# Both parts of the mixing stage's weight tiles made by transfers instead of ACT and DVE

## The chip, the cores and the metric

The kernel runs on one core of one Trainium2 chip. The metric is the time of one execution on the device in microseconds (us). A core has TensorE (PE, its weight loads shown as PEld), VectorE (DVE), ScalarE (ACT), GpSimd (POOL) and SyncE (SP). Each runs its own instructions in the order in which they stand, and waits on semaphores for the others. SP, ACT and POOL can issue transfers (DMAs); these run on 16 shared transfer engines.

## The reference

One decoder layer on 512 tokens of width 1024. Two token mixers run in parallel on the normalised input `h`: a sparse attention A, whose keys are the best 128 per query by an indexer's score, and a stick-breaking attention B. Both are gated, merged and projected, and a squared-ReLU MLP follows.

```python
h = rmsnorm(x, g_pre_mix[l]) * (1.0 + sc1) + sh1
proj = h @ w_in[l]
qa, ka, va, qb, kb, vb, qi, ki, wi, gate_a, gate_b = jnp.split(proj, split_at, axis=-1)
...
oa, ob = token_mixers(qa, ka, va, qb, kb, vb, qi, ki, wi)
merged = sigmoid(gate_a) * (oa @ w_up_a[l]) + sigmoid(gate_b) * (ob @ w_up_b[l])
x = x + ga1 * rmsnorm(merged @ w_out[l], g_post_mix[l])
...
u = relu(h @ w_ff1[l])
x = x + ga2 * rmsnorm((u * u) @ w_ff2[l], g_post_ffn[l])
```

## The kernel before

**Three products for one.** Matrices are multiplied in TensorE's `fp32r` format, which keeps fewer bits than fp32. To keep precision, each operand is split into a high part (the value rounded to fp32r) and a low part (what the rounding left), and `mm3` adds three products: high by high, high by low, low by high. `split` makes the parts: ACT copies the fp32 source into the high tile (a line of its own, L109), and DVE subtracts the high tile from the source into the low tile (L110).

**Weight tiles.** A weight tile is 128 partitions by up to 1024 columns, 512 KB. `wload` issues its load on SP's queue into a staging buffer `st` (three buffers) and splits it into `whi` and `wlo`, for each of which there are four buffers (`WBUF = 4`). A buffer is free when TensorE has done its last matmul with the tile four places earlier.

**The stages.** From 0 to 58 us the first stage multiplies `h` with `w_first` (indexer queries and keys and a part of V). Then comes the mixing stage, with 30 weight tiles in the order of the list `srcs`: six tiles of V weights (`w_v`) in two groups of three (V1 to V3 and V4 to V6: 876, 876 and 584 columns), and then, in the order of the string `ORDER`, two tiles (one of queries, one of keys) for each `b`, one for each `g` (gates), and four for each `a`. A group of V weights is used whole for each of four token blocks in turn, so its three buffers come free only in the last block. `wnext` hands out the next tile and calls `wload` for one tile ahead (`AHEAD = 1`). After the mixing stage, `srcs` goes on with the other gate tiles, `w_up` and `w_out`, and the MLP follows.

**What runs beside.** Into this stream of projections the generator tasks weave the indexer (scores, then 16 rounds of MAX and MATCH_REPLACE on DVE for the top-k), attention B (scores on TensorE; two sigmoids `a` and `be` on ACT; on DVE a scan of `a` and the product into `be`; transposes back on TensorE; `pT` evacuated by ACT) and later attention A. POOL makes masks and the three `affine_select`s on the indexer's scores `isc`, nothing else.

**Order.** The first stage's order is written by hand. In the mixing stage the order on each engine comes from a scheduler that works with its own estimates of durations; an engine then keeps to that order, whatever really comes late.

Of the kernel before, what the change touches and what calls it, by code (L numbers as in the profile page):

```python
# [7 lines left out]
F32 = mybir.dt.float32  # L8
F32R = mybir.dt.float32r
BF16 = mybir.dt.bfloat16  # L10
AF = mybir.ActivationFunctionType
ALU = mybir.AluOpType
# [3 lines left out]
D = 1024  # L16
# [45 lines left out]
def layer_kernel(tc, x, ada, vecs, c_row, rope, w_first, w_v, w_b, w_a, w_gate, w_up, w_out, w_ff1, w_ff2, out):  # L62
    nc = tc.nc
    es = ExitStack()
    with es:
# [5 lines left out]
        def uid(name):  # L71
            cnt[0] += 1
            return f"{name}_{cnt[0]}"
# [29 lines left out]
        def stage(src, w=D):  # L103
            st = per.tile([P, D], F32, name=uid("st"), tag="st", bufs=3)
            nc.sync.dma_start(st[:, :w], src)
            return st

        def split(dst_hi, dst_lo, src):
            nc.scalar.activation(dst_hi, src, AF.Copy)  # L109
            nc.vector.tensor_tensor(dst_lo, src, dst_hi.bitcast(F32), op=ALU.subtract)  # L110
# [1 line left out]
        wmore = []  # L112
        turn, wturn = [0], [0]

        def wload(src, w=D):
            st = stage(src, w)
            pool, tag, nb = per, "", WBUF
            if wmore:
                wturn[0] = (wturn[0] + 1) % (WBUF + 1)
                if wturn[0] == 0:  # L120
                    pool, tag, nb = wmore[0], "x", 1
            hi = pool.tile([P, D], F32R, name=uid("whi"), tag="whi" + tag, bufs=nb)
            lo = pool.tile([P, D], F32R, name=uid("wlo"), tag="wlo" + tag, bufs=nb)
            split(hi[:, :w], lo[:, :w], st[:, :w])
            return hi, lo

        def scaled_gain(dst, j, g0):
# [134 lines left out]
        for k in range(KT):  # L262
            if k + 1 < KT:
                prepare(k + 1)
            hi, lo = wfirst[k]
# [223 lines left out]
        srcs = [(w_v[g, i, :, :(k1 - k0) * VREST], (k1 - k0) * VREST) for g in range(2) for i, (k0, k1) in enumerate(V_CUTS)]  # L489
        feeds = {"b": iter(w_b[i] for i in range(8)), "g": iter(w_gate[i] for i in range(8)), "a": iter(w_a[i] for i in range(8))}  # L490
        for kind in ORDER:
            srcs += [(next(feeds[kind]), D) for _ in range({"b": 2, "g": 1, "a": 4}[kind])]
        for m in range(KT):
            srcs += [(w_gate[KT + m], D), (w_up[m], D)]
        srcs += [(w_out[k], D) for k in range(WOB)]
        ready = []

        def wnext(i=[0]):
            while len(ready) < min(len(srcs), i[0] + 1 + AHEAD):
                ready.append(wload(*srcs[len(ready)]))  # L500
            i[0] += 1
            return ready[i[0] - 1]

# [10 lines left out]
        def pair_b(hp):  # L514
            qq = q_pair()
            kk = k_pair()
            ps = yield from cols_T(wnext())
            for e in range(2):
                r, o = slice(e * HD, (e + 1) * HD), slice((1 - e) * HD, (2 - e) * HD)
                nc.scalar.activation(qq[r, e], ps[r], AF.Copy, scale=QK_SCALE)  # L520
                nc.vector.scalar_tensor_tensor(qq[o, e], ps[r], QK_SCALE, qq[r, e].bitcast(F32), op0=ALU.mult, op1=ALU.subtract)  # L521
            yield
            ps = yield from cols_T(wnext())
            for e in range(2):
                r, o = slice(e * HD, (e + 1) * HD), slice((1 - e) * HD, (2 - e) * HD)
                nc.scalar.activation(kk[r, 2 * e], ps[r], AF.Copy)
                nc.scalar.activation(kk[o, 2 * e + 1], ps[r], AF.Copy)
                nc.vector.tensor_tensor(kk[r, 2 * e + 1], ps[r], kk[r, 2 * e].bitcast(F32), op=ALU.subtract)
                evac(kk[o, 2 * e], kk[r, 2 * e + 1].bitcast(F32))
            yield  # L530
            tens[f"b{hp}"] = [(qq[:, e], kk[:, 2 * e:2 * e + 2]) for e in range(2)]

        def project(dst, scale):
            ws = [wnext(), wnext()]
            for t in range(NT):
                ts = slice(t * P, (t + 1) * P)
                ps = bank("mm")
                for k in range(KT):
                    hi, lo = ws[k // 4]
                    cs = slice((k % 4) * 256, (k % 4 + 1) * 256)  # L540
                    mm3(ps[:, :256], hTh[k][:, ts], hTl[k][:, ts], hi[:, cs], lo[:, cs], k == 0, k == KT - 1)
                    if k == 3:
                        yield
                nc.scalar.activation(dst[:, t], ps[:, :256], AF.Copy, scale=scale)  # L544
                if t == NT - 1:
                    do_rope(dst.rearrange("p t (h d) -> p t h d", h=4), 4)
                yield
# [104 lines left out]
        for m in range(KT):  # L652
# [3 lines left out]
            hi, lo = wnext()  # L656
# [50 lines left out]
        for k in range(KT):  # L707
            if k < WOB:
                wo.append(wnext())
            else:  # L710
                st = stage(w_out[k])
                hi = wp.tile([P, D], F32R, name=f"woh{k}")
                lo = wp.tile([P, D], F32R, name=f"wol{k}")
# [78 lines left out]
        def ff1(m, w, t0, t1):  # L792
# [8 lines left out]
            nc.vector.tensor_tensor(u2[m][:, cs], u2[m][:, cs], u2[m][:, cs], op=ALU.mult)  # L801

        ws = [wload(w_ff1[m]) for m in range(EARLY)]
        for h in range(2):
            for m in range(EARLY):
                ff1(m, ws[m], 2 * h, 2 * h + 2)
        for m in range(EARLY, MF):
            ff1(m, wload(w_ff1[m]), 0, NT)
            if m % 2 and m >= MF - 2 * KT:
                i = (m - MF + 2 * KT) // 2  # L810
                ada_cols(40 + i)
                gated_gain(KT + i, 40 + i, 72 + i)
# [106 lines left out]
```

## Time and profile before

| | |
|---|---|
| median of 3 runs | 812.72 us (812.08 to 813.03) |
| profiled execution | 811.92 us, its span 810.1 us |
| PE busy | 786.3 us, 97% of the span |
| DVE busy | 511.0 us, 63% |
| ACT busy | 363.0 us, 45% |
| POOL busy | 2.8 us |

The span runs from the first to the last instruction of the profiled execution; times in rows count from its start. An engine that is busy 97% on average can still stand in one stage, so the windows of a stage say more than the average. In a row `out<-in` names the written and the read tiles, and the bracket at its end gives the idle time before it and what ended it. A matmul's row shows a longer time than its distance to the next, since matmuls overlap.

### The profile page before, as it was taken

Reading aid. Unit: us, or ns where it says so; the run is one execution under the profiler, and the core shown is the slowest. Engines: PE = TensorE matmul, PEld = TensorE weight load, DVE = VectorE, ACT = ScalarE, POOL = GpSimd, SP = SyncE. Lnnn points to the kernel's source line nnn. Section 1 sums busy time; section 2 is a strip of 40 time slices with the busy share of each in tenths; the row PEclk is TensorE's granted clock in tenths of the full one; section 3 lists DMA queues with packets and bytes.
Section 4 is the critical chain, followed back from the end, with each engine's and each line's share of the span. In section 5 each row is a group of like instructions: output and inputs, shape, how many; then the busy total and the mean of one; then the engine's idle time right before and its main releaser. Section 6 shows DMA issues by size and latency. Waiting matters only on the chain.

```text
span 810.1 us, 10809 instructions
## 1 busy us (share of the span) xinstructions
PE 786.3 (97%) x4110; PEld 656.4 (81%) x4110; DVE 511.0 (63%) x973; ACT 363.0 (45%) x684; POOL 2.8 (0%) x15
## 2 busy tenths in 40 slices
PE   6999999989999999999999999999999999999996
PEld 5889977658889887887688998888888888888885
DVE  6876799999956776788767863344433433333325
ACT  6555657464546677631347753223322322332322
POOL 0000000000000000000000000000000000000000
PEclk9999999999999999999999999999999999999999
DMA  9933201122121210578780332344442232233202
GB/s 356 377 117 104 78 27 53 56 75 79 60 98 53 79 53 27 163 264 256 248 315 28 123 127 89 131 138 137 141 156 99 83 105 89 93 104 104 79 1 104
DMA packets 27987, 98.58 MB, mean 122 GB/s; under 512 B 3360, under 2 KB 3360, under 8 KB 27936
## 3 DMA queue, kind: packets, MB, share of 16 engines
q1 hardware_dynamic: 27216, 96.82, 35.2%
q10 hardware_dynamic: 720, 1.08, 0.4%
q8 instruction: 32, 0.52, 0.3%
q14 instruction: 19, 0.16, 0.1%
HBM read 95.79 MB, written 2.10 MB: 121 GB/s over the span
## 4 chain that ended last, share of the span: by engine, by line
PE 76%; DVE 15%; DMA 6%; issue 2%; ACT 2%; DVEq 0%; SPq 0%; ACTq 0%
PE mm L137 30%; PE s L137 27%; PE o L137 9%; PE tr L137 7%; DMA st<-in_ada_dram 3%; DVE a L483 3%; DVE isc L409 2%; DVE sm L408 2%; DVE wlo L110 2%; DMA st<-in_w_up_dram 2%; PE tr L427 1%; DVE be L485 1%; DVE st L210 1%; PE tr L333 1%; DVE qT L521 1%
## 5 line engine op out<-in xcount | busy, mean ns | idle before, releaser
L109 ACT ACTIVATE whi<-st 128x1024 fp32r<-128x1024 f32 (+2 forms) x122 | 127.5, 1047 | 180.8 <-PE mm L137 45.3
L110 DVE TENSOR_TENSOR wlo<-st,whi 128x1024 fp32r<-128x1024 f32 (+2 forms) x122 | 147.1, 1209 | 92.2 <-ACT whi L109 91.9
L137 PE MATMUL mm<-hTh,whi 128*128 128x512 f32 x192 | 78.7, 410 | 0.1
L110 DVE TENSOR_TENSOR ul<-u,uh 128x512 fp32r<-128x512 f32 x32 | 22.2, 692 | 89.7 <-ACT uh L109 89.6
L137 PE MATMUL mm<-hTh,wlo 128*128 128x512 f32 x192 | 75.6, 394 | 0.0
L137 PE MATMUL mm<-hTl,whi 128*128 128x512 f32 x192 | 75.4, 393 | 0.0
L109 ACT ACTIVATE uh<-u 128x512 fp32r<-128x512 f32 x32 | 20.2, 631 | 108.7 <-PE o L137 105.1
L137 PE MATMUL mm<-whi,hTh 128*128 128x256 f32 (+2 forms) x208 | 62.3, 306 | 0.1
L137 PE MATMUL mm<-whi,hTl 128*128 128x256 f32 (+2 forms) x208 | 60.2, 296 | 0.0
L137 PE MATMUL mm<-wlo,hTh 128*128 128x256 f32 (+2 forms) x208 | 60.1, 295 | 0.0
L210 DVE CUSTOM_DVE_ANT_0 st<-st,cb,vec 128x1024 f32<-128x1024 f32 x32 | 40.9, 1282 | 29.1 <-DMA st<-in_ada_dram 29.0
L137 PE MATMUL s<-h2h,whi 128*128 128x512 f32 (+1 forms) x144 | 52.7, 366 | 0.0
L137 PE MATMUL s<-h2l,whi 128*128 128x512 f32 (+1 forms) x144 | 52.6, 366 | 0.0
L137 PE MATMUL s<-h2h,wlo 128*128 128x512 f32 (+1 forms) x144 | 52.6, 366 | 0.0
L137 PEld LDWEIGHTS mm<-hTh,wlo 128*128 128x128 f32 x192 | 36.3, 189 | 7.8
L137 PEld LDWEIGHTS mm<-hTh,whi 128*128 128x128 f32 x192 | 36.5, 190 | 6.6 <-DVE qT L521 0.3
L137 PEld LDWEIGHTS mm<-hTl,whi 128*128 128x128 f32 x192 | 36.5, 190 | 6.2
L137 PEld LDWEIGHTS mm<-wlo,hTh 128*128 128x128 f32 x208 | 39.5, 190 | 1.0
L137 PEld LDWEIGHTS mm<-whi,hTl 128*128 128x128 f32 x208 | 39.5, 190 | 0.6
L137 PEld LDWEIGHTS mm<-whi,hTh 128*128 128x128 f32 x208 | 39.0, 190 | 0.7 <-ACT ka L544 0.3
L137 PE MATMUL mm<-h2h,wlo 128*128 128x512 f32 (+1 forms) x96 | 35.7, 372 | 0.0
L137 PE MATMUL mm<-h2h,whi 128*128 128x512 f32 (+1 forms) x96 | 35.7, 371 | 0.0
(296 smaller groups left out, 1755.1 us busy)
## 6 DMA issues: line engine op xcount, KB each, us to landing
st<-in_w_ff_dram SPq DMA_DIRECT2D x64, 512.0 KB, 3.3
st<-in_ada_dram SPq DMA_DIRECT2D x32, 512.0 KB, 4.2
sa<-in_ada_dram SPq DMA_DIRECT2D x16, 512.0 KB, 8.1
st<-in_w_gate_dram SPq DMA_DIRECT2D x16, 512.0 KB, 3.3
st<-in_w_first_dram SPq DMA_DIRECT2D x8, 512.0 KB, 8.5
st<-in_w_b_dram SPq DMA_DIRECT2D x8, 512.0 KB, 3.3
st<-in_w_a_dram SPq DMA_DIRECT2D x8, 512.0 KB, 3.2
st<-in_w_up_dram SPq DMA_DIRECT2D x8, 512.0 KB, 4.3
```

The source lines that it names most:

```text
L109: nc.scalar.activation(dst_hi, src, AF.Copy)
L110: nc.vector.tensor_tensor(dst_lo, src, dst_hi.bitcast(F32), op=ALU.subtract)
L137: nc.tensor.matmul(o, lhsT, rhs, start=start, stop=stop)
L210: nc.vector.tensor_tensor_reduce(out=st, in0=st, in1=cb[0], scale=1.0, scalar=vec[:, j:j + 1], op0=ALU.mult, op1=ALU.add, accum_out=mod[:, ...
L333: nc.tensor.transpose(ps[:, t * P:(t + 1) * P], s[:, t, i:i + 2].rearrange("p a d -> p (a d)"), identr)
L408: nc.vector.max(out=m8, in_=cur)
L409: nc.vector.match_replace(out=cur, in_to_replace=m8, in_values=cur, imm_value=SENT)
L427: nc.tensor.transpose(tr[:, j * P:(j + 1) * P], ps[e][:, j * P:(j + 1) * P], ident)
L483: nc.vector.tensor_tensor_scan(a[:, n - 1::-1], a[:, n - 1::-1], zero.to_broadcast([P, n]), 1.0, op0=ALU.mult, op1=ALU.add)
L485: nc.vector.tensor_tensor(be[:, :n - 1], be[:, :n - 1], a[:, 1:n], op=ALU.mult)
L521: nc.vector.scalar_tensor_tensor(qq[o, e], ps[r], QK_SCALE, qq[r, e].bitcast(F32), op0=ALU.mult, op1=ALU.subtract)
```

## The change

For the 30 tiles of the mixing stage `wload` takes another way. POOL issues a transfer from DRAM straight into the high tile, which casts fp32 to fp32r. ACT writes the negated high tile into the low tile. POOL issues a second transfer of the same source into the low tile that adds, so that source minus high stands there. No staging buffer, no load on SP and no subtraction on DVE belong to these tiles any more. All other tiles stay as they were. In `wnext` the tile's place in the list (`n_mixing` is 30) chooses the way.

```diff
-        def wload(src, w=D):
-            st = stage(src, w)
+        def wload(src, w=D, by_dma=False):
             pool, tag, nb = per, "", WBUF
...
             hi = pool.tile([P, D], F32R, name=uid("whi"), tag="whi" + tag, bufs=nb)
             lo = pool.tile([P, D], F32R, name=uid("wlo"), tag="wlo" + tag, bufs=nb)
-            split(hi[:, :w], lo[:, :w], st[:, :w])
+            if by_dma:
+                nc.gpsimd.dma_start(hi[:, :w], src)
+                nc.scalar.activation(lo[:, :w], hi[:, :w].bitcast(F32), AF.Copy, scale=-1.0)
+                nc.gpsimd.dma_start(lo[:, :w], src, accum_op=ALU.add)
+            else:
+                st = stage(src, w)
+                split(hi[:, :w], lo[:, :w], st[:, :w])
             return hi, lo
...
+        n_mixing = len(srcs)
...
-                ready.append(wload(*srcs[len(ready)]))
+                ready.append(wload(*srcs[len(ready)], len(ready) < n_mixing))
```

The order of instructions moves at two places that matter here. The first is POOL's queue around the V weights. Before, POOL had these rows from the start masks on:

```order
L94 MEMSET zero 128x1
L96 MEMSET eps 128x1
L344 MEMSET mask 128x128
L345 AFFINE_SELECT mask<-mask 128x128
L402 AFFINE_SELECT isc_585<-isc_585 128x128 x3
L915 UNCONDITIONAL_BRANCH
```

Now (`whi_614`, `whi_619`, `whi_624` are V1 to V3, and the `wlo` numbers one higher are their low parts; `629` and `823` are V4 and V5):

```order
L96 MEMSET eps 128x1
L124 DMA whi_614<-in_w_v_dram 128x876
L124 DMA whi_619<-in_w_v_dram 128x876
L126 DMA wlo_615<-in_w_v_dram 128x876
L349 MEMSET mask 128x128
L350 AFFINE_SELECT mask<-mask 128x128
L126 DMA wlo_620<-in_w_v_dram 128x876
L124 DMA whi_624<-in_w_v_dram 128x584
L126 DMA wlo_625<-in_w_v_dram 128x584
L124 DMA whi_629<-in_w_v_dram 128x876
L126 DMA wlo_630<-in_w_v_dram 128x876
L124 DMA whi_823<-in_w_v_dram 128x876
```

The high part of V3 stands behind the low part of V2, which in turn waits for ACT's negation. At the same place on ACT, at the end of the first stage, these rows stood before (`whi_622` is V2, `whi_628` is V3; `qi` evacuates the first stage's sums):

```order
L109 ACTIVATE whi_616<-st_614 128x876
L109 ACTIVATE whi_622<-st_620 128x876
L257 ACTIVATE hf_538<-tr_529,mod,g_92 128x512
L109 ACTIVATE hTh_105<-hf_538 128x512
L109 ACTIVATE whi_628<-st_626 128x584
L275 ACTIVATE qi_170<-mm_171 128x512
```

Now the negations of V2 and V3 stand right ahead of the same evacuations:

```order
L125 ACTIVATE wlo_615<-whi_614 128x876
L262 ACTIVATE hf_538<-tr_529,mod,g_92 128x512
L109 ACTIVATE hTh_105<-hf_538 128x512
L125 ACTIVATE wlo_620<-whi_619 128x876
L125 ACTIVATE wlo_625<-whi_624 128x584
L280 ACTIVATE qi_170<-mm_171 128x512
```

Each negation waits for a transfer, and what stands behind it on ACT waits too. The second place is TensorE at the start of the second V group, in its first token block. Before, the first matmul with the low part of V5 (`829` and `830`; V4 is `634`) came right behind the one with its high part:

```order
L137 MATMUL mm_845<-whi_634,hTl_108 128x292
L137 MATMUL mm_845<-whi_829,hTh_101 128x292
L137 MATMUL mm_845<-wlo_830,hTh_101 128x292
L137 MATMUL mm_845<-whi_829,hTl_109 128x292
L137 MATMUL s_858<-kTi,qTi_764 128x256 x2
L137 MATMUL s_864<-kTi,qTi_764 128x384 x2
L137 MATMUL s_870<-kTi,qTi_764 128x512 x2
L137 MATMUL mm_845<-whi_829,hTh_102 128x292
```

Now the low part of V5 (`824`; its high part is `823`, V4 is `629` and `630`) is first used after two rounds of the indexer's scores `s`, the transposes and the V4 matmuls of the second block (`mm_891`). The first of the two rounds is right behind the first use of the high part:

```order
L142 MATMUL mm_838<-whi_629,hTl_108 128x292
L142 MATMUL mm_838<-whi_823,hTh_101 128x292
L142 MATMUL s_851<-kTi,qTi_760 128x256 x2
L142 MATMUL s_857<-kTi,qTi_760 128x384 x2
L142 MATMUL s_863<-kTi,qTi_760 128x512 x2
L338 MATMUL tr_883<-identr,qs_820 128x128 x3
L142 MATMUL mm_891<-whi_629,hTh_98 128x292
L142 MATMUL mm_891<-wlo_630,hTh_98 128x292
```

And this is the end of that piece, six rows further on:

```order
L142 MATMUL mm_891<-whi_629,hTl_108 128x292
L142 MATMUL mm_891<-whi_823,hTh_101 128x292
L142 MATMUL s_904<-kTi,qTi_814 128x256 x2
L142 MATMUL s_910<-kTi,qTi_814 128x384 x2
L142 MATMUL s_916<-kTi,qTi_814 128x512
L142 MATMUL mm_838<-wlo_824,hTh_101 128x292
L142 MATMUL mm_838<-whi_823,hTl_109 128x292
```

Here the first use of the low part of V5 has moved behind other work, and the rest of the block (`mm_838`) with it. Elsewhere TensorE's order is nearly as it was.

## Rows read from the trace of the kernel before

**Rows 1.** The page: busy us (share) and instructions; PE's slices in tenths.

```profile
PE 786.3 (97%) x4110; PEld 656.4 (81%) x4110; DVE 511.0 (63%) x973; ACT 363.0 (45%) x684; POOL 2.8 (0%) x15
...
PE   6999999989999999999999999999999999999996
```

**Rows 2.** Windows: length, then busy us and count by engine, clock, DMA share, GB/s.

```profile
60.00:110.00 50.00, 50.00 (x324) 46.45 (x323) 36.83 (x71) 27.95 (x61) 1.15 (x3) 1.00 0.26 85
110.00:220.00 110.00, 102.88 (x616) 83.05 (x615) 108.81 (x238) 64.10 (x151) 0.00 (x0) 0.98 0.18 58
220.00:330.00 110.00, 109.99 (x708) 91.26 (x707) 75.36 (x216) 71.89 (x167) 0.00 (x0) 1.00 0.19 63
...
182.00:184.00 2.00, 1.48 (x7) 1.48 (x8) 2.00 (x4) 1.23 (x4) 0.00 (x0) 0.60 0.29 72
184.00:186.00 2.00, 2.00 (x7) 1.57 (x6) 2.00 (x4) 0.49 (x1) 0.00 (x0) 0.55 0.53 199
```

**Rows 3.** Waits from 110 to 220 us: us in total, times, longest us.

```profile
ACT a L481 <- DVE be L485: 15.1, 10, 3.7
...
PEld tr L427 <- ACT pT L182: 6.2, 4, 2.6
```

**Rows 4.** Timeline of PE around 180 us: start, us, operation.

```profile
179.93 0.39 PE L137 MATMUL mm<-hTh,wlo 128*128 128x512 f32 x1
182.52 1.54 PE L427 MATMUL tr<-identr,be 128*128 128x128 f32 x6 [2.20 <-ACT pT L182]
```

**Rows 5.** Timeline of DVE, near 74 and near 181 us.

```profile
73.91 0.55 DVE L184 CAST qTi<-tr 128x384 fp32r<-128x384 f32 x1
...
181.10 1.21 DVE L110 TENSOR_TENSOR wlo<-st,whi 128x1024 fp32r<-128x1024 f32 x1
```

**Rows 6.** Windows of DVE's instructions that write `wlo` alone.

```profile
110.00:220.00 110.00, 14.50 (x12) 0.98 0.18 58
```

**Rows 7.** DMA issues: times, KB each, median us to landing.

```profile
st<-in_w_first_dram SPq DMA_DIRECT2D x8, 512.0 KB, 8.5
st<-in_w_b_dram SPq DMA_DIRECT2D x8, 512.0 KB, 3.3
...
st<-in_w_v_dram SPq DMA_DIRECT2D x4, 438.0 KB, 3.9
...
st<-in_w_v_dram SPq DMA_DIRECT2D x2, 292.0 KB, 2.8
vec<-in_vecs_dram SPq DMA_DIRECT2D x1, 44.0 KB, 2.0
```

**Rows 8.** Timeline of POOL: its shortest instruction.

```profile
0.24 0.10 POOL L909 MEMSET const-float32-0.0<- 128x1 f32 x1 [0.24 <-issue]
```

**Rows 9.** Timeline of ACT, 48 to 57 us: V2, V3, then `qi`.

```profile
48.16 0.94 ACT L109 ACTIVATE whi<-st 128x876 fp32r<-128x876 f32 x1 [1.59 <-PE tr L137]
...
53.39 0.69 ACT L109 ACTIVATE whi<-st 128x584 fp32r<-128x584 f32 x1 [2.96 <-PE tr L137]
56.79 1.09 ACT L275 ACTIVATE qi<-mm 128x512 f32<-128x512 f32 x2 [2.71 <-PE mm L137]
```

**Rows 10.** Timeline of PE: lo V3, hi V5, scores and the next, lo of a key tile.

```profile
60.49 0.29 PE L137 MATMUL mm<-wlo,hTh 128*128 128x292 f32 x1
...
74.59 0.30 PE L137 MATMUL mm<-whi,hTh 128*128 128x292 f32 x1
74.73 0.29 PE L137 MATMUL mm<-wlo,hTh 128*128 128x292 f32 x1
...
74.99 1.21 PE L137 MATMUL s<-kTi,qTi 128*128 128x256 f32 x6
76.04 0.30 PE L137 MATMUL mm<-whi,hTh 128*128 128x292 f32 x1
...
101.02 0.39 PE L137 MATMUL mm<-hTh,wlo 128*128 128x512 f32 x1
```

**Rows 11.** Timeline of ACT: copies of V5, V6 and the first key tile.

```profile
70.23 0.94 ACT L109 ACTIVATE whi<-st 128x876 fp32r<-128x876 f32 x1 [0.76 <-PE mm L137]
...
72.49 0.69 ACT L109 ACTIVATE whi<-st 128x584 fp32r<-128x584 f32 x1 [0.19 <-PE mm L137]
...
88.43 1.06 ACT L109 ACTIVATE whi<-st 128x1024 fp32r<-128x1024 f32 x1 [0.82 <-PE mm L137]
```

## The prediction

> **What bounds the kernel now.** I read the busy table of the page first, then the windows by stage, then the waits of the stretch that stood out, and last the single rows around TensorE's gaps. PE is busy 97% of the span and DVE 63% [rows 1], so for most of the program a DVE instruction less buys nothing. The windows show one exception: from 110 to 220 us DVE is busy 108.8 of 110 us while PE's row shows 7.1 us of idle; from 220 to 330 us DVE drops to 75.4 and PE has no idle at all [rows 2]. 110 to 220 us is where the indexer's top-k (MAX and MATCH_REPLACE) is woven between the weight subtractions and the stick-breaking scans. The waits of that stretch name the chain: ACT waits for DVE's `be` 15.1 us in ten places, and TensorE's transposes wait for ACT's `pT` 6.2 us [rows 3]. The largest of these gaps shows how. TensorE issues its last matmul at 179.93 and the next transpose at 182.52, after an idle of 2.20 us [rows 4]; at 181.10 DVE was in the middle of a `wlo` subtraction of 1.21 us [rows 5], one of the instructions that the change takes away. Behind that gap the granted clock is 0.60 and 0.55 in two windows of 2 us [rows 2], the mean of stretches at 2.4 GHz and at 1.2 GHz: 0.8 + 0.9 = 1.7 us more.
>
> After 330 us nothing of the change is left, and every slice of PE but the last stands at 9 tenths or more [rows 1]; so a microsecond won or lost before 330 moves the end by one.
>
> **What it removes.** 30 subtractions on DVE. Twelve lie in the stretch from 110 to 220 us and take 14.5 us of it [rows 6]. The most that their going can give is the idle of TensorE there, 110 - 102.9 = 7.1 us, and the 1.7 us at half clock: 8.8 us. 14.5 us of relief in a stretch that loses 8.8 is enough to make DVE early at each gap, at least 1.2 us per tile. I keep the part that the waits tie to this chain: 6.2 of the 7.1 us, and the 1.7, less 0.4 for places where ACT now waits for a transfer: **7.5 us won**. The other 18 subtractions lie where TensorE doesn't wait; they give nothing. ACT's copy becomes a negation of the same shape and length: nothing either way. SP's 30 loads were staged ahead and are hidden now; their going gives nothing, and the three staging buffers that come free serve tiles whose first use is far off.
>
> **What it adds.** 60 transfers on POOL, which had 15 short instructions in all [rows 1]. Before, the load into staging ran ahead of the buffer's release, and from release to ready a tile cost one ACT copy and one DVE subtraction. Now release starts a chain: casting transfer, negation, accumulating transfer. No row shows a transfer issued by POOL, nor one that adds. The bounds come from the transfers of the trace: the same V weights on SP's queue land in 3.9 us (438 KB) and 2.8 us (292 KB), and the slowest load, in the crowded first stage, takes 8.5 us [rows 7]. That is 2.8 to 8.5 us for each of the two. Within that I take SP's own durations plus 1.0 us for POOL to make and issue each one, between the 0.10 us of POOL's shortest instruction [rows 8] and the 2.0 us that the smallest whole transfer takes [rows 7]. The adding transfer reads its target too. From 44 KB in 2.0 us to 512 KB in 3.3 us [rows 7] is 2.8 ns per KB, so a second read costs 1.2 us (438 KB) or 0.8 us (292 KB). So casting: 4.9 and 3.8 us; adding: 6.1 and 4.6 us.
>
> *First group of V weights (V1 to V3).* POOL's order is hi V1, hi V2, lo V1, mask, lo V2, hi V3, lo V3: the queue holds hi V3 back until the negation of V2 is done. V2's buffer is free at 48.16 [rows 9]; hi lands at 53.1; ACT's negation takes 0.94 (the copy's row) to 54.0; lo V2 is issued until 55.0; hi V3 lands at 58.8; its negation of 0.69 [rows 9] ends at 59.5, and holds the `qi` evacuations behind it on ACT, which started at 56.79 [rows 9]; lo V3 lands at 64.1. TensorE wants it at 60.49 [rows 10]. **3.6 us lost**, the late evacuations included, since TensorE waits for these inside the same gap. With SP's bare durations it lands at 59.7: nothing lost. With 8.5 us each, 16.8 us.
>
> *Second group (V4 to V6).* Four buffers and groups of three: only V4 finds a buffer early, V5 and V6 get their buffers only as the first group ends, at 70.23 and 72.49 [rows 11], and TensorE wants hi V5 at 74.59 [rows 10]. All that follows is moved by the 3.6 us alike, so I reckon in the old times. hi V5 lands at 75.1 (0.5 us late), the negation ends at 76.1, lo V5 lands at 82.2. The new order of TensorE puts work between the first use of hi V5 and that of lo V5: six score matmuls (1.05 us, the distance of rows 74.99 and 76.04 [rows 10]), three transposes, ten matmuls at the distance of rows 74.59 and 74.73 [rows 10], five more scores: 3.5 us. It wants lo V5 at 78.7 and gets it at 82.2: 3.5 more, **4.0 us lost**. Bare durations: 0.9; 8.5 us each: 10.1. V6 (fewer columns) is ready at 81.7, before its turn.
>
> *Clock.* Both gaps are longer than the one at 180 us, which brought 1.7 us of loss at half clock; twice 1.7: **3.4 us lost** (0 with bare durations).
>
> *Later tiles.* The next tightest is the first key tile: free at 88.43 [rows 11], its lo wanted at 101.02 [rows 10], 12.6 us; the chain takes 4.3 + 1.06 + 5.7 = 11.1. It holds, and every later tile has more room. The `isc` selection on POOL stands behind the load of the fifth query or key tile, which is released before `isc` is ready: no loss.
>
> **Sum.** 3.6 + 4.0 + 3.4 - 7.5 = +3.5 us. The profiled execution took 811.92 us (span 810.1); that gives 815.4. The median of the runs is 0.8 us above it: 816.
>
> With x us added to each POOL transfer the two gaps cost about 1.7 + 6x us and the clock up to 3.4; the change breaks even near x = 0.5.
>
> The row of V's transfers says 3.9 us on SP's queue [rows 7]. The Trainium skill, "DMA: Bandwidth & Descriptors", section "Specifications", gives the software path that POOL uses about 1 us to the first byte and the hardware path about 0.6, an x of 0.4. By that page the gaps cost 4.1, and the sum with 3.4 for the clock is 0 us. No run here shows it yet.
>
> **Rivals.**
> 1. *Faster: POOL's transfers are as quick as SP's.* For it: from 60 to 330 us the transfer engines are busy 18 to 26% [rows 2], and the bytes are the same. Against: three chained transfers must each be at the lower bound. The first gap vanishes, the second is 0.9 to 2.3 us, the clock 0 to 1.7, the full 8.8 is won: 4.5 to 8 us faster, about 807.
> 2. *Much slower: the adding transfer is slow, 8.5 us.* Place: the same gaps and the tile at 88.43. Loss 7.5 + 6.4 + 1.3 + 3.4 - 7.5 = +11: 824. It decides from about 6 us per adding transfer on. For it: it reads two places and writes one of them. Against: the queues are empty here, not crowded as they were at 8.5.
> 3. *No gain from DVE.* The gaps of 110 to 220 us stay, because ACT's in-order queue, with negations that wait for transfers, takes DVE's place. 3.6 + 4.0 + 3.4 = +11: 824. Against: ACT is busy only 64 of these 110 us [rows 2].
> 4. *POOL starved by DVE.* Between the issues that POOL makes for V5 and V6, DVE runs casts of 0.55 us [rows 5]; if an issue waits until such an instruction ends, six of them cost 3 us: 819. The Trainium skill, "SBUF — State Buffer", section "Who interferes with whom", says so: a DVE copy, cast or scaling in its two-port mode locks out POOL's making of descriptors. No run here shows it.
>
> **Chances.** The forecast with its own range of 811 to 820 has 0.42; rival 1 0.28; rival 2 0.15; rivals 3 and 4 0.15. The measurement tells 0.2% (1.6 us) from no change. Rival 1 is faster nearly throughout; of the forecast's range some 0.03 is faster, 0.14 within 0.2% and 0.25 slower; of the last two about 0.02 is within it. Faster 0.30, same 0.16, slower 0.54. Range: from rival 1's 806 up to 830, over rivals 2 and 3 and part of the way to the bound of 8.5 us for both transfers (16.8 + 10.1 + 3.4 - 7.5 = +23, before what later tiles add).
>
> **What would show it.** Right: two gaps of TensorE of 3 to 5 us in front of `wlo` matmuls of V weights, near 61 and 82 us, each followed by a stretch at half clock; behind them the program some 11 us late, and at 220 us only 3 to 4 us late, with DVE visibly idle between 110 and 220 us and the transposes' wait for `pT` gone. Wrong: casting transfers well under 4.5 us and adding ones under 5 (then it is faster), adding ones over 6 us, or gaps left between 110 and 220 us.

## The result, and the profile after

The changed kernel takes 826.16 us (median of 4 runs, 824.42 to 827.89) against 812.46 for the kernel before: ratio 1.0168, interval 1.0145 to 1.0191. It is 13.7 us slower. The forecast was 816, the range 806 to 830. The direction and the range held, the size did not: 10 us of the loss were not foreseen, and 826 lies above the 811 to 820 that the forecast gave itself.

The page after, with the rows that answer to [rows 1]; the last is the queue of the transfers that POOL issues (packets, MB, share of the 16 engines' span):

```profile
PE 791.0 (96%) x4110; PEld 659.7 (80%) x4110; DVE 481.3 (59%) x943; ACT 364.5 (44%) x684; POOL 46.0 (6%) x75
...
PE   6989898898999999999999999999999999999996
...
q0 software_dynamic: 8640, 29.95, 16.6%
```

The windows of the three stretches, in the columns of [rows 2]:

```profile
60.00:110.00 50.00, 46.85 (x299) 43.93 (x300) 23.28 (x50) 27.31 (x62) 11.28 (x16) 0.93 0.60 128
110.00:220.00 110.00, 101.60 (x563) 80.31 (x562) 101.37 (x237) 63.15 (x145) 17.69 (x26) 0.97 0.52 117
220.00:330.00 110.00, 109.10 (x739) 93.07 (x738) 65.09 (x203) 69.25 (x164) 11.77 (x16) 1.00 0.44 104
```

From 60 to 110 us TensorE now stands for 3.2 us and runs at a granted clock of 0.93: the V gaps. From 110 to 220 us it stands for 8.4 us, where it stood for 7.1 [rows 2]. DVE lost the twelve subtractions of that stretch, 14.5 us [rows 6], and the stretch that was to win 7.5 us got worse. (The program is about 9 us late by then, so the window holds somewhat earlier work than before; the table below compares the same work.)

The transfers, in the columns of [rows 7] (KB each, median us from issue to landing):

```profile
whi<-in_w_v_dram POOLq DMA_DIRECT2D x4, 438.0 KB, 3.7
wlo<-in_w_v_dram POOLq DMA_DIRECT2D x4, 438.0 KB, 5.4
...
whi<-in_w_v_dram POOLq DMA_DIRECT2D x2, 292.0 KB, 4.5
wlo<-in_w_v_dram POOLq DMA_DIRECT2D x2, 292.0 KB, 4.9
```

Matching each weight tile's first matmul in the two traces shows where the time goes (the traced run of the changed kernel took 824.42 us, its span 822.6). The mixing tiles are numbered 1 to 30 here (V1 to V6 are 1 to 6, the first query tile is 7); the same for the experiments (us late against the kernel before; a minus is early):

| kernel | tile 7 | tile 14 | tile 18 | tile 30 |
|---|---|---|---|---|
| changed kernel | 8.9 | 15.5 | 12.8 | 12.2 |
| e1: V the old way | -0.5 | 8.9 | 3.0 | 3.5 |
| e2: V alone by transfers | 13.1 | 13.1 | 12.7 | 12.9 |
| e7: hi first | 0.0 | 9.0 | 3.1 | 2.3 |
| e6b: short subtraction | 0.4 | 5.9 | -1.1 | -0.9 |
| e9: short subtraction, old order | -0.1 | -1.2 | -7.7 | -8.9 |
| e11: before, moved order | 0.3 | 9.7 | 5.0 | 7.0 |
| e8: 24 by transfers, old order | 1.9 | 14.7 | 12.1 | 23.3 |
| e12: 12 by transfers, late negations | -0.2 | -1.4 | -8.7 | -10.5 |

So the V tiles cost 8.9 us, and tiles 7 to 30 cost another 3.3 instead of bringing 7.5.

### The profile page after: what moved, and what is told of

Same layout as the page of the kernel before. It is cut to its first block, busy times and chain, and to the rows that moved or that the text cites. A ratio compares the mean times of both kernels' runs of the same rounds, so it can differ in the third digit from the quotient of the medians.

```text
span 822.6 us, 10842 instructions
## 1 busy us (share of the span) xinstructions
PE 791.0 (96%) x4110; PEld 659.7 (80%) x4110; DVE 481.3 (59%) x943; ACT 364.5 (44%) x684; POOL 46.0 (6%) x75
## 4 chain that ended last, share of the span: by engine, by line
PE 72%; DMA 10%; DVE 9%; issue 5%; ACT 3%; POOL 1%; DVEq 0%; SPq 0%; POOLq 0%; ACTq 0%
PE mm L142 27%; PE s L142 26%; PE o L142 9%; PE tr L142 6%; DMA st<-in_ada_dram 2%; PE tr L432 2%; DMA st<-in_w_gate_dram 2%; DMA whi<-in_w_v_dram 2%; DVE st L215 1%; DVE a L488 1%; DVE sm L413 1%; DMA whi<-in_w_b_dram 1%; DVE isc L414 1%; DVE wlo L110 1%; DVE be L490 1%
## 5 line engine op out<-in xcount | busy, mean ns | idle before, releaser
L109 ACT ACTIVATE whi<-st 128x1024 fp32r<-128x1024 f32 x92 | 96.8, 1054 | 165.2 <-PE s L142 44.8
L110 DVE TENSOR_TENSOR wlo<-st,whi 128x1024 fp32r<-128x1024 f32 x92 | 112.4, 1224 | 81.1 <-ACT whi L109 80.9
L142 PE MATMUL mm<-wlo,hTh 128*128 128x256 f32 (+2 forms) x208 | 61.8, 303 | 2.5 <-DMA wlo<-in_w_v_dram 2.5
L125 ACT ACTIVATE wlo<-whi 128x1024 fp32r<-128x1024 f32 (+2 forms) x30 | 30.7, 1022 | 30.9 <-DMA whi<-in_w_v_dram 10.4
L142 PE MATMUL s<-kT,qT 128*128 128x256 f32 (+2 forms) x128 | 30.8, 346 | 5.2 <-ACT be L487 4.4
```

What stands on the lines that cost most here:

```text
L125: nc.scalar.activation(lo[:, :w], hi[:, :w].bitcast(F32), AF.Copy, scale=-1.0)
L142: nc.tensor.matmul(o, lhsT, rhs, start=start, stop=stop)
```

## The experiments

Theory A, with which I began, was the third rival of the prediction: ACT, in order, waits for the casting transfer in front of each negation, and that takes DVE's place. Rows of ACT in the changed kernel between 108 and 130 us, and one of PE, speak for it:

```profile
114.83 1.06 ACT L125 ACTIVATE wlo<-whi 128x1024 fp32r<-128x1024 f32 x1 [3.91 <-DMA whi<-in_w_b_dram]
...
123.12 1.06 ACT L125 ACTIVATE wlo<-whi 128x1024 fp32r<-128x1024 f32 x1 [3.93 <-DMA whi<-in_w_b_dram]
...
125.49 0.28 ACT L486 ACTIVATE a<-s 128x128 f32<-128x128 f32 x1
125.67 0.27 ACT L487 ACTIVATE be<-s 128x128 f32<-128x128 f32 x1
```

```profile
125.99 0.50 PE L142 MATMUL s<-kT,qT 128*128 128x256 f32 x2 [1.80 <-ACT be L487]
```

The sigmoids stand behind the second negation (and a table load of 1.28 us), and TensorE's next scores wait 1.80 us for them; behind that gap the granted clock is 0.75 from 126 to 128 us and 0.50 from 128 to 130. At this gap the trace itself shows Theory A's wait. Whether it makes the whole loss was to be tested.

**e1 and e2: the two parts apart.** e1 splits V the old way and brings the other 24 tiles by transfers; e2 is the reverse.

```diff
-                ready.append(wload(*srcs[len(ready)], len(ready) < n_mixing))
+                ready.append(wload(*srcs[len(ready)], 6 <= len(ready) < n_mixing))   # e1
+                ready.append(wload(*srcs[len(ready)], len(ready) < 6))               # e2
```

> The six tiles of V weights are split by ACT and DVE as before the change; the other 24 mixing tiles keep the two transfers and the negation. Theory A (the V tiles' chain of transfers costs 9.4 us at the two group starts, the other 24 tiles cost 3 us more because ACT stands still behind negations that wait for their transfer): the time falls by about 9.4 us to 816-817, still 3 us above the kernel before, with gaps of TensorE left between 110 and 220 us. Rival B (the later gaps are an after-effect of the late start of the top-k and go when the V gaps go): 805 to 810, as DVE's relief is won.

> Only the six V tiles use the two transfers; the other 24 are split by ACT and DVE as before the change. Theory A: the two gaps at the V groups and the half clock behind them alone, about 812.5 + 9.4 = 822, with the gaps of 110 to 220 us as in the kernel before. Rival B (the losses come with the late tiles, the V gaps are refilled by later slack): 812 to 815.

e1 took 817.35 us, 1.0054 [1.0036, 1.0072]; e2 825.82, 1.0156 [1.0141, 1.0171]. e1 is just above Theory A's place: without the V gaps the change still loses. e2's loss is all there by tile 7 and 4 us more than expected. Its first stage ends 0.8 us later than before, and an SP load of 7.6 us now runs beside the adding transfer of V6, which takes 7.9 us (5.4 in the changed kernel); V6 brings a gap of its own (3.09 us at 90.64). The losses of e1 and e2 therefore don't add up to that of the whole change.

**e3 and e4: POOL does the arithmetic.** e3 is the changed kernel with the negation on POOL, to free ACT; e4 the kernel before with the 30 subtractions on POOL, to free DVE without transfers.

```diff
-                nc.scalar.activation(lo[:, :w], hi[:, :w].bitcast(F32), AF.Copy, scale=-1.0)
+                nc.gpsimd.tensor_scalar(lo[:, :w], hi[:, :w].bitcast(F32), -1.0, None, op0=ALU.mult)   # e3
...
-            nc.vector.tensor_tensor(dst_lo, src, dst_hi.bitcast(F32), op=ALU.subtract)
+            nc.gpsimd.tensor_tensor(lo[:, :w], st[:, :w], hi[:, :w].bitcast(F32), op=ALU.subtract)     # e4
```

> As the change, but POOL instead of ACT writes the negated high part, so that no ACT instruction waits for a transfer. Theory A (ACT's waiting took DVE's gain of 7.5 us away and added 3): the gaps of 110 to 220 us shrink from about 11 to under 3 us, the V gaps stay or grow by a few us with a slower negation: 815 to 819. Rival C (the subtractions on DVE never were what TensorE waited for): the gaps of 110 to 220 us stay near 9 us and the time is 823 to 830.

> The kernel before, with the subtraction of the 30 mixing tiles moved from DVE to POOL; loads and ACT copies as before. It takes the same 30 instructions off DVE and adds no transfer and no wait on ACT. Theory A (DVE's relief is worth up to 8.8 us): 804 to 808 if POOL's subtraction is under 4 us, with TensorE's idle of 110 to 220 us near zero. Rival C (relief is worth nothing): 811 to 814. If POOL's subtraction takes much longer than DVE's 1.2 us, the V groups start late and some of the gain is lost.

853.17 us, 1.0472 [1.0433, 1.0511], and 833.12, 1.0244 [1.0228, 1.0259]: both miss every forecast, and neither tells the theories apart, since each brought a cost of its own on POOL. POOL's negation takes 2.8 us and its subtraction 2.4 (the last section), and in e4 DVE's own instructions grew.

**e5 and e7: the casting transfer one tile earlier.** If ACT's waits were the cause, this would remove them. V stays the old way; a tile's casting transfer is issued at the tile before, its negation and adding transfer follow at the next call. e5 puts the casting transfer behind the previous adding one on POOL's queue, e7 ahead of it:

```diff
+            if 6 <= i[0] and want < n_mixing and len(ready) == want:
+                ready.append(wload(*srcs[want], True))     # casting transfer alone; e5 has this behind the loop
+            while open_lo and len(ready) - len(open_lo) < want:
+                finish_lo()                                # negation and adding transfer
```

> The six V tiles are split the old way. The other 24 come by transfers, but each casting transfer is issued one tile earlier, and the negation and the adding transfer follow at the next tile, so that ACT should find the data there. Theory A (the 7.5 us were not won because ACT's in-order queue waits about 4 us in front of a negation for its casting transfer, and the evacuations behind it are late): ACT's waits for casting transfers all but vanish, the gaps of TensorE between 110 and 220 us go, and the time is 804 to 809 us. Rival B (TensorE's gaps in that stretch have another cause, such as the order in which ACT and DVE pass the score rows to each other, and DVE's subtractions were no part of them): 811 to 818 us even though ACT's waits are gone.

> As the kernel with the casting transfer issued one tile earlier, but now POOL's queue has it in front of the previous tile's adding transfer and not behind it. There a loop was left: the casting transfer of a tile stands behind an adding transfer that waits for the previous negation, and the next negation waits for the casting transfer, some 8 us a tile, about what TensorE needs for one. With the order turned the loop runs over two tiles. Theory A (ACT's waits for casting transfers, from this loop, ate the gain): these waits go and the time is 804 to 810 us. Rival B (the gaps come from something else): 814 to 818 us with the waits gone.

e5 took 816.62 us, 1.0037 [1.0022, 1.0052], e7 816.26, 1.005 [1.0025, 1.0074]. Neither tested what it was meant to: the negations still came up on ACT ahead of their transfers, and the waits did not go. Between 110 and 220 us ACT still waits 10.9 and 10.4 us for casting transfers, in e1 9.5. So they left open whether a freed DVE is worth anything at all, which the next run asked.

**e6b: DVE's relief by itself.** No transfer; the kernel before, with 24 subtractions cut to a quarter of their columns. All matmuls with the low parts of these tiles read that quarter, so three quarters of them are left out. (e6, a first form of it, gave no time.)

```diff
+                nc.vector.tensor_tensor(lo[:, :256], st[:, :256], hi[:, :256].bitcast(F32), op=ALU.subtract)
+                return hi, First(lo)     # reads of lo use its first columns
```

> The kernel before, with the DVE subtraction of the 24 mixing tiles after V cut to 256 of 1024 columns, and their lo part read from those columns alone: part of the computation is left out, in the same instructions of TensorE. No transfer is added and ACT does what it did. It measures the relief of DVE by itself, about 0.8 us for each of twelve tiles between 110 and 220 us. Theory A (DVE was the late one there): the 7 us of idle and the half clock shrink, 804 to 808 us. Rival B (DVE's relief is worth nothing, TensorE's gaps have another cause): 811 to 814 us.

810.85 us, 0.998 [0.997, 0.9991]: 1.9 us, Rival B's side of it. A relief of 0.8 us (0.42 us for 1.21) for each of twelve tiles, where TensorE waits, moves the end by hardly anything. Its trace says why: tile 14 is 5.9 us later than before, behind a gap of 2.66 us at 144.59, which the kernel before does not have. The same gap stands in the changed kernel, 2.60 us at 155.78. These are ACT's rows ahead of it in the changed kernel:

```profile
150.37 1.21 ACT L187 ACTIVATE pT<-tr 128x384 f32<-128x384 f32 x4
153.85 0.59 ACT L532 ACTIVATE kT<-mm 64x512 fp32r<-64x512 f32 x1 [2.27 <-DVE kT L534]
154.46 0.59 ACT L533 ACTIVATE kT<-mm 64x512 fp32r<-64x512 f32 x1
155.07 0.38 ACT L486 ACTIVATE a<-s 128x256 f32<-128x256 f32 x1
```

and these the same instructions in the kernel before:

```profile
136.61 1.21 ACT L182 ACTIVATE pT<-tr 128x384 f32<-128x384 f32 x4
139.45 0.39 ACT L481 ACTIVATE a<-s 128x256 f32<-128x256 f32 x1 [1.62 <-DVE be L485]
139.73 0.38 ACT L482 ACTIVATE be<-s 128x256 f32<-128x256 f32 x1
139.99 0.39 ACT L481 ACTIVATE a<-s 128x256 f32<-128x256 f32 x1
140.25 0.41 ACT L482 ACTIVATE be<-s 128x256 f32<-128x256 f32 x1
140.52 1.09 ACT L109 ACTIVATE whi<-st 128x1024 fp32r<-128x1024 f32 x1
142.71 0.59 ACT L526 ACTIVATE kT<-mm 64x512 fp32r<-64x512 f32 x1 [1.11 <-DVE kT L528]
```

The order is another one. Before, the sigmoids `a` and `be`, which free the banks of the scores `s`, ran ahead of the key evacuation `kT`. Now `kT` stands ahead of them and waits 2.27 us for DVE's part of the keys, which stands among the top-k rounds; and TensorE's next scores wait for the sigmoids:

```profile
155.78 0.61 PE L142 MATMUL s<-kT,qT 128*128 128x384 f32 x2 [2.60 <-ACT be L487]
```

The scheduler, given a shorter subtraction (e6b) or none (the changed kernel), put ACT's and DVE's instructions in another order. This is Theory C: the order that comes with the change, not the work in it.

**e8 to e11: the order held fixed, or moved alone.** The order of one kernel was laid on another by dependencies between neighbours on TensorE, DVE and ACT, from the mixing stage on:

```diff
+        for a, b in zip(order, order[1:]):
+            tc.add_manual_dep(mine[b], mine[a].name, ..., reason="order")
```

> The kernel before with the 24 subtractions cut to 256 of 1024 columns (part of the computation left out, as in the run with the scheduler's own order), and the order of the kernel before kept on TensorE, DVE and ACT. Nothing but DVE's relief, 0.8 us a tile, is left. Theory C: without the moved order the relief shows, 804 to 807 us. Rival D (the relief is worth little even so): 809 to 812 us.

> The kernel before, complete, with full subtractions and no transfers added, but on TensorE, DVE and ACT in the order that the scheduler gave the kernel with short subtractions. It prices the moved order by itself. Theory C: 815 to 818 us, with the gap of 2 to 3 us in front of scores near 145 us that the kernel before has not. Theory A: the order is no matter, 812 to 813.5 us.

> The kernel with the V tiles split the old way and the other 24 tiles by transfers, but with the order of the kernel before kept on TensorE, DVE and ACT from the mixing stage on: each negation stands where the copy into the high tile stood, and the subtractions are gone. POOL's order is the scheduler's. Theory C (the scheduler, given no subtractions, moved instructions of ACT and DVE, among them evacuations of key sums ahead of sigmoids, and this order made new gaps that ate the gain): 804 to 809 us. Theory A (ACT waits for casting transfers, whatever the order): 813 to 819 us, with the waits of ACT for transfers still there.

> The whole changed kernel, all 30 tiles by transfers, in the order of the kernel before on TensorE, DVE and ACT. Theory C: the loss at the V tiles stays, 9 us or somewhat more since the old order wants the low part of V5 sooner, and the gain of 4 to 8 us behind 110 us appears: 814 to 820 us. Theory A: no gain behind 110 us, 822 to 828 us.

e9, e6b's work in the old order, takes 804.48 us, 0.9895 [0.9874, 0.9915]: 8.4 us faster. e11, the full old work in e6b's order, takes 820.5, 1.0095 [1.0075, 1.0116]: 7.7 slower, with the gap. Windows of e9, then of e11, from 110 to 220 us, and e11's gap:

```profile
110.00:220.00 110.00, 108.56 (x667) 87.86 (x667) 103.12 (x249) 67.56 (x157) 0.00 (x0) 1.00 0.21 68
```

```profile
110.00:220.00 110.00, 98.67 (x569) 78.41 (x568) 108.47 (x236) 61.45 (x141) 0.00 (x0) 0.97 0.17 53
```

```profile
148.46 0.65 PE L137 MATMUL s<-kT,qT 128*128 128x384 f32 x2 [3.43 <-ACT be L482]
```

Same work, other order: TensorE's idle there goes from 7.1 [rows 2] to 11.3 us. Same order, less work: to 1.4 us, with the clock at 1.00. The pair shows that e6b's relief of DVE is worth 8 us and that e6b's order takes most of it (e6b, with both, is 1.9 us faster; the two don't quite add up). e11's gap is 0.4 us beyond the 2 to 3 us and its time 2.5 us beyond the range that I had expected.

e8 and e10 show Theory A at work instead. They took 836.44 us, 1.0297 [1.0274, 1.032], and 849.13, 1.0458 [1.0434, 1.0483], worse than both theories said. In the old order a negation stands where the copy stood, right behind the release of its buffer, and there it must wait for a transfer that has only then been issued. Rows of POOL, then of ACT, in e8:

```profile
133.88 0.56 POOL L124 DMA_DIRECT2D whi<-in_w_b_dram  x1 [3.26 <-PE mm L142]
138.98 0.85 POOL L126 DMA_DIRECT2D wlo<-in_w_b_dram  x1 [4.54 <-ACT wlo L125]
143.00 0.55 POOL L124 DMA_DIRECT2D whi<-in_w_b_dram  x1 [3.17 <-PE mm L142]
```

```profile
137.63 1.06 ACT L125 ACTIVATE wlo<-whi 128x1024 fp32r<-128x1024 f32 x1 [4.21 <-PE s L142]
```

TensorE's last matmul with the buffer lets the casting transfer go at 133.88, and ACT, idle for 4.21 us, starts the negation at 137.63. (The bracket names the last event that the profile has; what was late is the transfer, which landed after 3.7 us.) From 110 to 220 us ACT stands so for 37.3 us in front of negations, in the changed kernel for 14.3. So the old order doesn't suit the transfers either: the copy could run at the release, the negation has to come later.

**e12: both causes taken away.** Only tiles 10 to 21 come by transfers; in the kernel before, their subtractions start between 95 and 194 us, ten of the twelve in the stretch. The old order is kept, but for the negations: each stands on ACT behind the landing of its transfer, on average 7 us (4.7 to 9.5) behind its issue (this is in the order list, which the diff leaves out). On POOL each casting transfer stands ahead of the previous tile's adding one.

```diff
-                ready.append(wload(*srcs[len(ready)], len(ready) < n_mixing))
+                ready.append(wload(*srcs[len(ready)], 9 <= len(ready) < 21))
...
+    for (_, lo), (hi, _) in zip(tc.moved, tc.moved[1:]):
+        tc.add_manual_dep(lo.ins, hi.ins.name, ..., reason="order")
```

> A complete kernel that aims below both. Only the twelve tiles whose DVE subtractions stand between about 92 and 190 us come by transfers; V and all others are split the old way. TensorE, DVE and ACT keep the order of the kernel before, but each of the twelve negations stands 7 to 11 us behind the release of its buffer on ACT, so that its casting transfer has landed, and on POOL each casting transfer stands ahead of the previous tile's adding one. Theory C (DVE's relief is worth 8 us where the order is kept, and the transfers themselves cost nothing once no engine waits for them): 803 to 807 us, DVE idle between 110 and 220 us, ACT's waits for transfers gone. Rival E (transfers, or 12 negations at other places on ACT, cost what DVE gives): 811 to 818 us.

801.37 us, 0.9871 [0.9854, 0.9889]: 11.2 us faster than the kernel before, below Theory C's range, and 25 below the changed kernel. Its windows:

```profile
60.00:110.00 50.00, 50.00 (x324) 46.52 (x323) 35.10 (x71) 27.51 (x60) 4.93 (x8) 1.00 0.36 106
110.00:220.00 110.00, 109.57 (x674) 89.06 (x673) 104.04 (x240) 69.48 (x160) 13.79 (x19) 1.00 0.51 116
```

TensorE stands for 0.4 us. Among ACT's waits there is none in front of a negation; the casting transfers land after 3.4 to 5.0 us, the adding ones after 5.2 to 8.1, and TensorE and ACT wait for none of them. DVE is still busy 104.0 of 110 us: it does not become visibly idle, as I had said it would; it is no longer late.

## Why the prediction was right in direction and wrong in size

- **First V group, "3.6 us lost": right in mechanism, and in size partly by luck.** TensorE stands for 3.08 + 0.33 = 3.4 us. The chain ran as worked out, with hi V3 behind lo V2 on POOL, and the `qi` evacuations behind V3's negation on ACT. But TensorE stood mostly for these evacuations, not for lo V3, and two errors cancelled: hi V2 landed after 3.8 us (4.9 estimated), hi V3, issued 0.6 us behind lo V2, only after 5.8 (3.8 estimated). Rows of ACT, then of PE; the last is the gap of the second group:

```profile
59.47 0.69 ACT L125 ACTIVATE wlo<-whi 128x584 fp32r<-128x584 f32 x1 [6.74 <-DMA whi<-in_w_v_dram]
60.07 1.06 ACT L280 ACTIVATE qi<-mm 128x512 f32<-128x512 f32 x2
```

```profile
60.70 0.40 PE L142 MATMUL mm<-whi,hTh 128*128 128x292 f32 x1 [3.08 <-ACT qi L280]
...
64.85 0.61 PE L142 MATMUL mm<-wlo,hTh 128*128 128x292 f32 x1 [0.33 <-DMA wlo<-in_w_v_dram]
...
85.29 0.41 PE L142 MATMUL mm<-wlo,hTh 128*128 128x292 f32 x1 [2.12 <-DMA wlo<-in_w_v_dram]
```

- **Second group, 4.0, and the clock, 3.4.** The gap in front of lo V5 is at the place foreseen, but 2.12 us: hi V5 landed after 3.5 us (4.9 estimated), lo V5 after 5.1 (6.1). The clock was right: 0.54 and 0.61 are granted between 62 and 66 us, 0.51 and 0.64 between 86 and 90, so each gap cost 1.7 us more. With the first stage 0.5 us earlier, V costs 8.9 + 0.5 = 9.4 us in all; the three terms said 11.0.
- **Transfer durations: near in the median.** Adding 5.4 and 4.9 us (6.1 and 4.6 estimated); casting 3.7 and 4.5 (4.9 and 3.8). The extra microsecond per POOL transfer is not in the casting ones of 438 KB, which land as SP's do [rows 7]; that much of rival 1 was right, and V lost 9.4 us all the same. The Trainium skill, "DMA: Bandwidth & Descriptors", section "Specifications", gives about 1 us to the first byte on the software path and about 0.6 on the hardware path; the 3.7 beside SP's 3.9 does not show this difference.
- **"7.5 us won" between 110 and 220 us: the step that failed.** The premise, that DVE is late there and that its relief is worth about that much, was right: e9 wins 8.4 us with nothing but the relief, e12 11.2. The step assumed that DVE would do less in an order that otherwise stays. I had compared TensorE's order, where little moves, and ACT's only around V; the section on the change therefore names two places and misses a third. ACT moved too, and e11 prices one such order, with full subtractions, at 7.7 us. And for the places where ACT waits for a transfer the term took off 0.4 us: ACT waits 14.3 us in front of negations there, and TensorE's gap at 125.99 alone is 1.80. The signs named for being right failed there as well: TensorE still stands for 8.4 us, and tile 22, which began at 220 us before, is 10.9 us late and not 3 to 4. That e12 wins 2 us more than the 8.8 that I had called the most is not explained here.
- **Rival 3 ("no gain from DVE") came nearest, 824, with half of its reason and some luck.** ACT does take DVE's place at the gaps, partly waiting for transfers, as it said (the gap at 125.99), and partly because of where its evacuations now stand (the gap at 155.78), which nothing in the prediction had. Its sum was the V terms alone, 11.0; these measured 9.4, and tiles 7 to 30 lost 3.3 more. How the missing gain of the changed kernel splits between the two causes isn't settled: e11's order is that of e6b, which shares the move shown above with the changed kernel but differs from it elsewhere, and no kernel had the changed kernel's transfers and order without its waits. e1 loses 6 us more than e6b with nearly the same gap ahead of tile 14 (2.63 and 2.66 us); that waits of 9.5 us on ACT are the reason is argued, not shown.
- **Rival 2, which said 824 too, did not happen** (adding transfers 4.9 to 5.6 us in the median, the longest 7.2, not 8.5), nor rival 4: POOL's issues take 0.53 to 0.88 us between 60 and 90 us, and no idle of POOL there is ended by DVE.
- **"Later tiles, 0": right for tiles 22 to 30,** which lose 1.3 us between them (10.9 late at tile 22, 12.2 at tile 30).
- **Loose figures that decided nothing.** The 6.2 us of [rows 3] are what the weight loads (PEld) waited; the matmuls waited 4.6 us for `pT` (`PE tr L427 <- ACT pT L182: 4.6, 3, 2.2`), by which the term would have been 5.9. By the steps written down, the first group loses 15.8 us and not 16.8 at 8.5 us each, and with SP's bare durations lo V3 lands at 59.3 (60.1 with the second read) and not at 59.7, still in time.

## What to carry to other kernels

When a scheduler sets the order, removing work from a busy engine also changes the order on every engine that it feeds; compare the order of the engine that the bottleneck waits for, not only of the bottleneck, and separate work from order with two runs: the new work in the old order, and the old work in the new. An in-order engine should meet an instruction that waits for a transfer only after the transfer has had its time: in e12 that was on average 7 us behind the issue, and the tiles had time enough for it. e8, without it, lost 24 us; e12, with it, for half the tiles and with another order on POOL, won 11 (no run prices the three apart). And replace only the work that stands in the bottleneck's way: the V tiles, where DVE had time and the buffers came late, paid 9 us for nothing.

## What the hardware showed that I had not expected

POOL's own arithmetic next to DVE is dear on both sides. In e4 the subtraction on POOL takes twice DVE's 1.21 us, and DVE's product `be` of two tiles grows from 679 ns to 1528, while MAX8 stays at 0.68 us. Rows of before, then of e4, POOL's and DVE's (POOL's group is of the whole run, DVE's of 110 to 225 us; busy us, mean ns):

```profile
L408 DVE MAX8 sm<-isc 128x8 f32<-128x512 f32 x15 | 10.3, 685 | 0.0
...
L485 DVE TENSOR_TENSOR be<-be,a 128x511 f32<-128x511 f32 x8 | 5.3, 679 | 0.0
```

```profile
L126 POOL TENSOR_TENSOR wlo<-st,whi 128x1024 fp32r<-128x1024 f32 (+2 forms) x30 | 72.2, 2415 | 209.0 <-ACT whi L125 202.1 <-PE s L141 6.9
```

```profile
L412 DVE MAX8 sm<-isc 128x8 f32<-128x512 f32 x16 | 10.9, 679 | 0.0
...
L489 DVE TENSOR_TENSOR be<-be,a 128x511 f32<-128x511 f32 x6 | 9.2, 1528 | 0.0
```

The Trainium skill, "SBUF — State Buffer", section "Who interferes with whom", says that a DVE instruction with two inputs in that memory contends with a POOL instruction that reads it, and that one with at most one input there doesn't, outside the modes that use two ports; these rows agree. POOL's transfers did nothing of the kind: in e12, with 24 of them, `be` takes 684 ns and MAX8 687; the price of the transfers that the runs show was the time until they land.
